# A two-layer diffusion backbone on one core: another order of loads and another sum of squares at its beginning

## The chip, the cores and the metric

The kernel runs on one core of a Trainium2 chip. Its time is the device time of one execution in microseconds (us), the median of several runs; smaller is better. The profile shows one execution, instruction by instruction, for the engines PE (TensorE matmul), PEld (TensorE weight load, which overlaps PE), DVE (VectorE), ACT (ScalarE), POOL (GpSimd) and SP (SyncE, which here only issues DMAs).

## The reference, cut to what matters

Two layers work on 256 latent and 256 context tokens of width 1024. Only the first half-step of the first layer matters here: a norm over the 1024 features of each token, a modulation with a scale and a shift that are themselves matrix products of a condition vector, and a gated FFN.

```python
def _rms(x, g):
    xf = x.astype(jnp.float32)
    y = xf * lax.rsqrt(jnp.mean(xf * xf, axis=-1, keepdims=True) + RMS_EPS)
    return (y * g.astype(jnp.float32)).astype(x.dtype)

def _half_ffn(x, gain, shift, scale, gate, w_gu, w_down):
    h = _rms(x, gain) * (1 + scale) + shift
    a, u = jnp.split(h @ w_gu, 2, axis=-1)
    return x + 0.5 * gate * ((jax.nn.silu(a) * u) @ w_down)
...
m_lat = [m[:, None, :] for m in jnp.split(jax.nn.silu(c) @ w_ada[l] + b_ada[l], N_MOD, axis=-1)]
```

## The kernel before

All is kept transposed: features on the 128 partitions, the 512 tokens (256 latent, then 256 context) along the free dimension, so that x is eight tiles of 128x512, one for each k of 0 to 7. A product in fp32 quality is made of three fp32r matmuls: the weight and the activation are split into a high and a low part, and `mm3` (L341 to L343) multiplies high by high, high by low and low by high. The weight's parts are made on the fly: a raw unit of 128x2048 lands in `raw`, ACT copies 512 columns of it to `whi` (L242), DVE subtracts to get `wlo` (L243). `Weights.piece` does that for a quarter of a unit; a quarter holds the weights for two k. The activation's parts are made by `split` (L346 on ACT, L347 on DVE).

What the first matmuls of the FFN need is made in `start` and `first`:

- `start` issues all early DMAs on SP, in the order x (eight of 256 KB, L398), the constants `cst` (L400, which hold the identity and a block of ones), `vec` (L401), and then `w_ada` for the modulation of feature block 0, 1 (L286, 1 MB each), the first raw unit (L219, 1 MB), `w_ada` 2, the second raw unit, `w_ada` 3 to 7.
- ACT squares the eight tiles of x (L429), DVE adds them into two running sums and these into `acc` (L432, L434). PE multiplies four 128-column slices of `acc` by one column of ones (L441, four matmuls of 128x1): that is the sum over the partitions. DVE turns it into the norm's factor with eleven small instructions (`rsqrt`, L353 to L362).
- `nbc` spreads the factor: two matmuls of 128x128 for each half of the tokens (L588), then an ACT copy out of the bank into `rb` in SBUF (L593).
- `first(j)` makes scale and shift of feature block j: eight matmuls on 32-column groups (L466), an ACT copy (L469), two matmuls with the selector `sel` (L471), two small DVE instructions into `mods` (L475, L476).
- `first_h(k)` makes the FFN's input of block k: DVE multiplies x by `rb` (L484), ACT applies scale and shift to the latent and the context half (L487, two instructions), `split` makes the two parts.

`first(0)` and `first(1)` are called in `start`; the FFN's first loop then runs over k: `first_h(k)`, `first(k + 2)`, and the matmuls of two weight units at once, twelve for each k, into four banks. Each engine works through its instructions in one fixed order; that order is settled when the program is built, by a scheduler which knows priorities and data dependences. A DMA waits for the eighth before it on the same kind of queue to land, since there are eight semaphores that take turns.

## Time and profile before

| | us |
|---|---|
| median of 3 runs | 2036.82 (2030.58 to 2037.09) |
| the profiled execution | 2033.4 |
| its span in the profile | 2031.7 |
| PE busy in the span | 1999.8 (98%) |
| DVE busy | 1394.2 (69%) |
| ACT busy | 884.0 (44%) |

PE is idle for 32 us of the span, and the largest piece of that lies at its start. Times of PE's instructions are read as distances between starts: matmuls overlap, so the duration of one is longer than its share of the engine. The column PEclk is the granted clock as a share of full speed, 1.00 for 2.4 GHz and 0.50 for 1.2 GHz. In the first stretches it reads 1.00 throughout, but the same 128x512 matmuls follow one another every 0.43 us until about 27 us and every 0.23 us from about 29 us on, which are the two levels; there the distances tell the level, not the column.

### The profile page before, as it was taken

To read this page: it belongs to the slowest core of one execution; us is meant where nothing else is said; L and a number is where in the kernel's file an instruction comes from. 1 tells how busy PE (TensorE), PEld (TensorE's weight loads), DVE (VectorE), ACT (ScalarE), POOL (GpSimd) and SP (SyncE) were. 2 spreads that over 40 slices of the span, in tenths; PEclk is the share of its full clock that TensorE was granted. 3 is DMA by queue.
4 is the path that set the end of the run, shared out by engine and by line. 5 is a ranking of instruction groups with operands and counts; after the bars stand their busy time and mean duration, and the time that the engine had idled before them with its cause. 6 is when DMAs were issued, how large, how long until landed. Compare 5 with 4: busy or idle time off the path is not lost.

```text
span 2031.7 us, 30903 instructions
## 1 busy us (share of the span) xinstructions
PE 1999.8 (98%) x12019; PEld 1751.9 (86%) x12019; DVE 1394.2 (69%) x2729; ACT 884.0 (44%) x1683; POOL 22.8 (1%) x49
## 2 busy tenths in 40 slices
PE   7999999999999999999999999999999999999997
PEld 4888888998888888988888898888889889999997
DVE  4999833577458746999933489933346877887675
ACT  4432333456453334532233353223335656466563
POOL 0000000000001000000000000000000000000000
PEclk9999999999999999999999999999999999999999
DMA  9566532324322464466732336532232434455553
GB/s 365 188 227 237 201 101 96 133 89 153 135 89 78 151 233 167 150 240 216 256 122 85 113 122 236 191 121 88 91 127 106 165 135 141 158 206 181 183 174 107
DMA packets 65125, 322.87 MB, mean 159 GB/s; under 512 B 7233, under 2 KB 9681, under 8 KB 36433
## 3 DMA queue, kind: packets, MB, share of 16 engines
q1 hardware_dynamic: 58896, 309.87, 43.9%
q10 hardware_dynamic: 6048, 11.01, 1.5%
q8 instruction: 94, 1.54, 0.3%
q14 instruction: 55, 0.44, 0.1%
q0 software_dynamic: 32, 0.01, 0.0%
HBM read 301.46 MB, written 19.40 MB: 158 GB/s over the span
## 4 chain that ended last, share of the span: by engine, by line
PE 92%; DVE 3%; DMA 2%; ACT 2%; issue 1%; SPq 0%; DVEq 0%; POOLq 0%; ACTq 0%
PE bank L341 28%; PE bank L342 27%; PE bank L343 27%; DMA raw<-in_w_out 1%; PE bank L1209 1%; PE bank L791 1%; PE bank L793 1%; PE bank L792 1%; PE bank L1237 1%; PE bank L1220 1%; DVE wlo L243 0%; PE bank L1236 0%; PE bank L1106 0%; DMA raw<-in_w_in 0%; PE bank L977 0%
## 5 line engine op out<-in xcount | busy, mean ns | idle before, releaser
L341 PE MATMUL bank<-blk,whi 128*128 128x512 f32 (+3 forms) x3064 | 1066.6, 349 | 3.2 <-ACT blk L346 2.6
L342 PE MATMUL bank<-blk,whi 128*128 128x512 f32 (+3 forms) x3064 | 1060.2, 346 | 0.4 <-DVE blk L347 0.3
L343 PE MATMUL bank<-blk,wlo 128*128 128x512 f32 (+3 forms) x3064 | 1059.0, 346 | 0.0
L243 DVE TENSOR_TENSOR wlo<-raw,whi 128x512 fp32r<-128x512 f32 (+2 forms) x748 | 500.5, 678 | 330.0 <-ACT whi L242 326.6
L242 ACT ACTIVATE whi<-raw 128x512 fp32r<-128x512 f32 (+2 forms) x748 | 458.7, 622 | 612.5 <-PE bank L342 564.2
L341 PEld LDWEIGHTS bank<-blk,whi 128*128 128x128 f32 (+1 forms) x3064 | 579.7, 189 | 79.0 <-issue 3.4
L342 PEld LDWEIGHTS bank<-blk,whi 128*128 128x128 f32 (+1 forms) x3064 | 580.4, 190 | 71.1 <-DVE blk L347 1.1
L343 PEld LDWEIGHTS bank<-blk,wlo 128*128 128x128 f32 (+1 forms) x3064 | 580.2, 189 | 70.9 <-DVE wlo L243 0.3
L523 DVE CUSTOM_DVE_ANT_0 blk<-blk,blk,vec 128x1024 f32<-128x1024 f32 x256 | 327.7, 1280 | 2.7 <-DMA blk<-in_w_ada 0.3
L346 ACT ACTIVATE blk<-blk 128x512 fp32r<-128x512 f32 (+2 forms) x128 | 71.5, 560 | 70.6 <-DVE blk L644 49.6
L347 DVE TENSOR_TENSOR blk<-blk,blk 128x512 fp32r<-128x512 f32 (+2 forms) x128 | 76.8, 601 | 27.1 <-ACT blk L346 24.7
L643 ACT ACTIVATE blk<-bank 128x512 f32<-128x512 f32 x66 | 39.5, 598 | 112.6 <-PE bank L343 112.6
L644 DVE TENSOR_TENSOR blk<-blk,bank 128x512 f32<-128x512 f32 x66 | 45.2, 685 | 53.4 <-PE bank L343 53.3
L664 DVE SCALAR_TENSOR_TENSOR blk<-bank,mods,blk 128x256 f32<-128x256 f32 x112 | 50.4, 479 | 33.3 <-PE bank L343 33.3
L342 PE MATMUL bank<-blk,blk 128*128 128x256 f32 (+1 forms) x195 | 58.6, 303 | 0.0
L343 PE MATMUL bank<-blk,blk 128*128 128x256 f32 (+1 forms) x195 | 58.2, 302 | 0.0
L341 PE MATMUL bank<-blk,blk 128*128 128x256 f32 (+1 forms) x195 | 57.9, 304 | 0.0
L498 ACT ACTIVATE blk<-blk 128x256 f32<-128x256 f32 (+1 forms) x55 | 26.1, 474 | 54.1 <-DVE blk L664 36.7
L342 PEld LDWEIGHTS bank<-blk,blk 128*128 128x128 f32 x195 | 37.1, 191 | 1.5
L343 PEld LDWEIGHTS bank<-blk,blk 128*128 128x128 f32 x195 | 37.0, 191 | 1.3
L341 PEld LDWEIGHTS bank<-blk,blk 128*128 128x128 f32 x195 | 36.5, 191 | 1.5
L607 ACT ACTIVATE blk<-blk,mods 128x256 f32<-128x256 f32 x64 | 34.9, 589 | 3.7 <-DVE blk L606 3.7
(254 smaller groups left out, 1395.5 us busy)
## 6 DMA issues: line engine op xcount, KB each, us to landing
raw<-in_gu SPq DMA_DIRECT2D x88, 1024.0 KB, 4.9
blk<-in_w_ada SPq DMA_DIRECT2D x72, 1024.0 KB, 4.8
raw<-in_dn SPq DMA_DIRECT2D x64, 704.0 KB, 4.1
raw<-in_w_in SPq DMA_DIRECT2D x42, 1024.0 KB, 4.8
raw<-in_w_out SPq DMA_DIRECT2D x8, 1024.0 KB, 6.8
dx<-blk SPq DMA_DIRECT2D x16, 256.0 KB, 2.2
raw<-in_w_a SPq DMA_DIRECT2D x4, 1024.0 KB, 6.1
raw<-in_pm SPq DMA_DIRECT2D x3, 1024.0 KB, 4.8
```

The lines of the kernel that those rows point to most:

```text
L242: self.nc.scalar.activation(h[:, a:b], r[:, a:b], AF.Copy)
L243: self.latest = self.nc.vector.tensor_tensor(lo[:, a:b], r[:, a:b], h[:, a:b].bitcast(F32), ALU.subtract)
L341: mm(o, wh, xh, start=start, stop=False)
L342: mm(o, wh, xl, start=False, stop=False)
L343: mm(o, wl, xh, start=False, stop=stop)
L346: self.nc.scalar.activation(hi, src, AF.Copy)
L347: return self.nc.vector.tensor_tensor(lo, src, hi.bitcast(F32), ALU.subtract)
L523: v.tensor_tensor_reduce(self.junk.f, w[:, 1024 * i:1024 * i + 1024], self.cb.f[:, 1024 * s:1024 * s + 1024], 1.0, ba, ALU.mult, ALU.add, ...
L607: nc.scalar.activation(t.f[:, c], t.f[:, c], AF.Identity, bias=self.mod(l, ms, i, s), scale=self.mod(l, mg, i, s))
L643: nc.scalar.activation(t.f[:, :n], o[0][:, :n], AF.Silu)
L644: nc.vector.tensor_tensor(t.f[:, :n], t.f[:, :n], o[1][:, :n], ALU.mult)
L664: nc.vector.scalar_tensor_tensor(self.x[m].f[:, c], p[:, c], self.mod(l, gm, m, s), self.x[m].f[:, c], ALU.mult, ALU.add)
```

## The change

The FFN's loops stay as they are. What changes lies in `start`, `first_h` and the order of loads:

- x comes from two queues: tiles 0, 2, 4, 6 are issued by SP, tiles 1, 3, 5, 7 by ACT.
- The loads after x stand in another order: `cst`, `w_ada` 0, `vec`, the first halves of both raw units, `w_ada` 1, the second half of the first unit, `w_ada` 2, the second half of the second unit, `w_ada` 3 to 7.
- ACT's table is loaded for a one-column Silu that needs no DMA; the Silu of the condition comes after the squares.
- ACT squares tiles 0, 2, 4, 6, DVE tiles 1, 3, 5, 7. DVE adds only two pairs (4 with 5, 6 with 7). The other sums are made by PE: each of the six terms is multiplied by the column of ones in four matmuls, all accumulated in one bank (24 matmuls instead of four).
- The norm's factor is spread by four matmuls into one bank of its own (`banks[7]`), and L499 of the new kernel (L484 before) reads it from there. The two ACT copies are gone.
- In `first_h` the context half gets its scale and shift from DVE (L501), not ACT.

```diff
-            self.nc.sync.dma_start(r[:, :n], ap)
+            h = n // 2 if u < self.halves else n
+            self.nc.sync.dma_start(r[:, :h], ap[:, :h])
...
-            nc.sync.dma_start(self.x[k].f, I["x"][:, k])
+            (nc.scalar if k % 2 else nc.sync).dma_start(self.x[k].f, I["x"][:, k])
...
-        nc.sync.dma_start(self.vec[:, :V_N], I["vec"][:, :V_N])
...
-            if k == 1:
+            if k == 0:
+                nc.sync.dma_start(self.vec[:, :V_N], I["vec"][:, :V_N])
                 self.W.open(self.raw[:1], list(zip(self.whi, self.wlo)))
-            elif k == 2:
                 self.W.more(self.raw[1])
+            elif k < 3:
+                self.W.rest(k - 1)
...
+        nc.vector.memset(self.tiny[:, 0:1], 0.0)
+        nc.scalar.activation(self.tiny[:, 1:2], self.tiny[:, 0:1], AF.Silu)
...
-        self.acc, odd = self.A.get(), self.A.get()
-        two = [self.acc, odd]
+
+        ps, sq = self.ax_bank(), []
         for k in range(KD):
-            t = two[k] if k < 2 else self.A.get()
-            nc.scalar.activation(t.f, self.x[k].f, AF.Square)
-            if k > 1:
-                a = two[k % 2].f
-                nc.vector.tensor_tensor(a, a, t.f, ALU.add)
-                self.A.free(t)
-        nc.vector.tensor_tensor(self.acc.f, self.acc.f, odd.f, ALU.add)
-        self.A.free(odd)
+            sq.append(self.A.get())
+            if k % 2:
+                nc.vector.tensor_tensor(sq[k].f, self.x[k].f, self.x[k].f, ALU.mult)
+            else:
+                nc.scalar.activation(sq[k].f, self.x[k].f, AF.Square)
+            if k in (5, 7):
+                nc.vector.tensor_tensor(sq[k].f, sq[k - 1].f, sq[k].f, ALU.add)
+        nc.scalar.activation(st[:, :, 0:2], self.cc.rearrange("p (k s) -> p k s", s=2), AF.Silu)
+        terms = (0, 1, 2, 3, 5, 7)
+        for k in terms:
+            for t in range(4):
+                nc.tensor.matmul(ps[:, t:t + 1], sq[k].f[:, 128 * t:128 * t + 128], self.ones[:, 0:1], start=(k, t) == (0, 0), stop=k == 7, skip_group_check=True)
...
-        ps = self.ax_bank()
-        for t in range(4):
-            nc.tensor.matmul(ps[:, t:t + 1], self.acc.f[:, 128 * t:128 * t + 128], self.ones[:, 0:1], start=True, stop=True)
...
+        self.rb = self.banks[7]
         with self.tc.issue_after(mm.ins):
-            self.nbc(0)
-            self.nbc(1)
+            for t in range(4):
+                c0 = 8 + 4 * (t // 2) + t % 2
+                nc.tensor.matmul(self.rb[:, t * 128:t * 128 + 128], bc(self.tiny[:, c0], 1, 128), self.ident, start=True, stop=True)
...
-        nc.vector.tensor_tensor(t.f, self.x[j].f, self.rb.f, ALU.mult)
-        for s in range(2):
-            c = slice(256 * s, 256 * s + 256)
-            nc.scalar.activation(t.f[:, c], t.f[:, c], AF.Identity, bias=self.mod(0, 0, j, s), scale=self.mod(0, 1, j, s))
+        nc.vector.tensor_tensor(t.f, self.x[j].f, self.rb, ALU.mult)
+        nc.scalar.activation(t.f[:, :256], t.f[:, :256], AF.Identity, bias=self.mod(0, 0, j, 0), scale=self.mod(0, 1, j, 0))
+        nc.vector.tensor_scalar(t.f[:, 256:], t.f[:, 256:], self.mod(0, 1, j, 1), self.mod(0, 0, j, 1), ALU.mult, ALU.add)
```

The lines move by 8 to 15: L441 is L450 afterwards, L466 is L481, L471 is L486, L588 of the beginning is L465, L475 and L476 are L490 and L491, L484 is L499, L487 is L500 (with L501 beside it), L341 to L343 are L349 to L351, L346 and L347 are L354 and L355, L242 and L243 are L250 and L251.

On PE, from the program's first matmul to the FFN's second weight unit, this stood in a row before (`bank_132` and `bank_133` are the first unit's two outputs, `bank_134` and `bank_131` the second's; `cstat` holds the Silu of the condition, and the tiles blk_158 to blk_160 hold w_ada 0 to 2):

```order
L441 MATMUL bank_136<-cst,blk_180 128x1 x4
L466 MATMUL bank_137<-blk_158,cstat 32x256 x8
L588 MATMUL bank_135<-cst,tiny 128x128 x2
L588 MATMUL bank_136<-cst,tiny 128x128
L471 MATMUL bank_137<-cst,blk_180 128x2 x2
L466 MATMUL bank_137<-blk_159,cstat 32x256 x8
L341 MATMUL bank_132<-blk_250,whi_141 128x512
L342 MATMUL bank_132<-blk_252,whi_141 128x512
L341 MATMUL bank_133<-blk_250,whi_141 128x512
...
L466 MATMUL bank_135<-blk_160,cstat 32x256 x8
```

and this stands there now (blk_157 to blk_159 hold w_ada 0 to 2):

```order
L450 MATMUL bank_136<-cst,blk_183 128x1 x16
L450 MATMUL bank_136<-cst,blk_188 128x1 x8
L481 MATMUL bank_137<-blk_157,cstat 32x256 x8
L465 MATMUL bank_138<-cst,tiny 128x128
L486 MATMUL bank_137<-cst,blk_230 128x2 x2
L465 MATMUL bank_138<-cst,tiny 128x128 x3
L349 MATMUL bank_132<-blk_268,whi_141 128x512
...
L351 MATMUL bank_132<-blk_268,wlo_143 128x512
L481 MATMUL bank_135<-blk_158,cstat 32x256 x8
L350 MATMUL bank_133<-blk_270,whi_141 128x512
```

The sum has 24 products instead of four, and `first(1)` (the second L466, now L481 on `bank_135`) has moved from ahead of the FFN's first matmul to behind its sixth. From the 131st of 11,111 PE instructions on (the 151st afterwards) both kernels have the same order on PE to the end.

On DVE, from the first use of the norm's factor on, this stood in a row before (`wlo_143` belongs to the first unit, `wlo_144` to the second; L484 makes the input of a block, L475 and L476 its scale and shift):

```order
L484 TENSOR_TENSOR blk_270<-blk_145,blk_180 128x512
L484 TENSOR_TENSOR blk_362<-blk_145,blk_180 128x512
L484 TENSOR_TENSOR blk_454<-blk_146,blk_180 128x512
L475 TENSOR_SCALAR mods_129<-bank_137,small,vec 128x2
L476 TENSOR_SCALAR mods_129<-bank_137,vec 128x2
L347 TENSOR_TENSOR blk_252<-blk_270,blk_250 128x512
```

and this stands there now:

```order
L499 TENSOR_TENSOR blk_288<-blk_145,bank_138 128x512
L251 TENSOR_TENSOR wlo_143<-raw_139,whi_141 128x512 x2
L501 TENSOR_SCALAR blk_288<-blk_288,mods_129 128x256
L251 TENSOR_TENSOR wlo_144<-raw_140,whi_142 128x512 x2
L355 TENSOR_TENSOR blk_270<-blk_288,blk_268 128x512
L499 TENSOR_TENSOR blk_320<-blk_145,bank_138 128x512
L490 TENSOR_SCALAR mods_129<-bank_135,small,vec 128x2
L491 TENSOR_SCALAR mods_129<-bank_135,vec 128x2
L251 TENSOR_TENSOR wlo_143<-raw_139,whi_141 128x512 x2
L501 TENSOR_SCALAR blk_320<-blk_320,mods_129 128x256
```

Two subtractions of weight parts (L251) now stand between the factor and L501 for the first block, and two more between the scale and shift of the second block (L490, L491) and its L501; before, the four of a unit stood together behind the first block's parts.

## Rows read from the trace of the kernel before

**Rows 1.** Waits of PE, whole span: waiter, releaser, us in total, times, longest.

```profile
PE bank L441 <- DVE blk L434: 12.8, 1, 12.8
```

**Rows 2.** Chain that ended last, 12 to 24 us: start, us, work.

```profile
12.77 1.88 PE bank L441 x8
17.08 1.65 PE bank L588 x6
...
19.37 0.65 PE bank L588 x2
20.05 0.39 ACT blk L593
```

**Rows 3.** Timeline, 4.5 to 21 us: start, us, engine, line, form, [idle before].

```profile
4.57 0.43 SPq L400 DMA_DIRECT2D cst<-in_cst  x1
...
11.87 0.17 DVE L438 TENSOR_SCALAR small<-vec 128x8 f32<-128x8 f32 x1
...
12.77 1.78 PEld L441 LDWEIGHTS bank<-cst,blk 128*128 128x128 f32 x8 [12.77 <-DVE blk L434]
...
14.67 0.16 DVE L443 TENSOR_SCALAR tiny<-bank 128x4 f32<-128x4 f32 x1 [1.96 <-PE bank L441]
...
16.86 0.16 DVE L362 SCALAR_TENSOR_TENSOR tiny<-tiny 128x4 f32<-128x4 f32 x1
...
19.94 1.94 PE L466 MATMUL bank<-blk,cstat 128*32 128x256 f32 x16
```

**Rows 4.** DMA issues around 4.5 us: KB each, us from issue to landing.

```profile
cst<-in_cst SPq DMA_DIRECT2D x1, 160.5 KB, 5.9
```

**Rows 5.** Stretches: length, busy time of PE, PEld, DVE, ACT, POOL; PEclk, DMA share, GB/s.

```profile
35.00:560.00 525.00, 525.00 (x2966) 442.53 (x2966) 365.40 (x690) 220.99 (x392) 4.22 (x8) 1.00 0.46 161
...
2.00:4.00 2.00, 0.00 (x0) 0.00 (x0) 0.00 (x0) 0.00 (x0) 0.00 (x0) 1.00 0.82 237
4.00:6.00 2.00, 0.00 (x0) 0.00 (x0) 0.00 (x0) 0.85 (x1) 0.00 (x0) 1.00 1.03 342
...
10.00:12.00 2.00, 0.00 (x0) 0.00 (x0) 2.00 (x6) 0.82 (x2) 0.00 (x0) 1.00 1.02 431
```

**Rows 6.** Chain that ended last, 672 to 690 us.

```profile
678.06 3.46 PE bank L1280 x24
...
685.99 0.43 PE bank L342
...
686.69 0.23 PE bank L341
```

**Rows 7.** One of the stretches there.

```profile
680.00:682.00 2.00, 2.00 (x10) 1.90 (x10) 0.44 (x2) 0.00 (x0) 0.00 (x0) 0.50 0.75 240
```

**Rows 8.** Timeline, 21 to 35 us.

```profile
23.64 0.80 PE L341 MATMUL bank<-blk,whi 128*128 128x512 f32 x1
...
24.79 0.80 PE L342 MATMUL bank<-blk,whi 128*128 128x512 f32 x1 [0.35 <-DVE blk L347]
...
25.25 2.49 DVE L243 TENSOR_TENSOR wlo<-raw,whi 128x512 fp32r<-128x512 f32 x4
...
34.73 0.61 PE L471 MATMUL bank<-cst,blk 128*128 128x2 f32 x4 [0.50 <-ACT blk L469]
```

**Rows 9.** Groups: line, engine, form, count; busy us, mean ns; idle before, releaser.

```profile
L664 DVE SCALAR_TENSOR_TENSOR blk<-bank,mods,blk 128x256 f32<-128x256 f32 x112 | 50.4, 479 | 33.3 <-PE bank L343 33.3
L475 DVE TENSOR_SCALAR mods<-bank,small,vec 128x2 f32<-128x2 f32 x8 | 2.2, 279 | 9.6 <-PE bank L471 9.6
L346 ACT ACTIVATE blk<-blk 128x512 fp32r<-128x512 f32 x9 | 5.6, 625 | 0.2
```

**Rows 10.** Chain that ended last, 40 to 43 us.

```profile
40.21 1.00 PE bank L466 x16
41.21 0.43 PE bank L342
...
42.34 0.34 PE bank L471 x4
```

More of the change, by code (lines that the diff above doesn't have):

```diff
@@ L164, in __init__ @@
         self.lent = None
+        self.halves = 2
         self.latest = NULL
@@ L174, in open, with rest @@
         self.plan()
+    def rest(self, u):
+        if self.order:
+            r, n = self.at[u][:2]
+            self.nc.sync.dma_start(r[:, n // 2:n], self.src(u)[:, n // 2:])
     def more(self, raw):
@@ L406, in start @@
             self.AW.more(self.abuf[k].f)
-            if k == 1:
+            if k == 0:
+                nc.sync.dma_start(self.vec[:, :V_N], I["vec"][:, :V_N])
                 self.W.open(self.raw[:1], list(zip(self.whi, self.wlo)))
-            elif k == 2:
                 self.W.more(self.raw[1])
+            elif k < 3:
+                self.W.rest(k - 1)
         nc.sync.dma_start(self.cst[:, 321:], I["cst"][:, 321:])
         nc.sync.dma_start(self.vec[:, V_N:], I["vec"][:, V_N:])
+        nc.vector.memset(self.tiny[:, 0:1], 0.0)
+        nc.scalar.activation(self.tiny[:, 1:2], self.tiny[:, 0:1], AF.Silu)
         nc.vector.memset(self.cstat, 0.0)
         st = self.cstat.rearrange("p (k s) -> p k s", s=32)
-        nc.scalar.activation(st[:, :, 0:2], self.cc.rearrange("p (k s) -> p k s", s=2), AF.Silu)
         self.st = st
@@ L424, in start @@
         self.Sr = [self.cstr[:, 128:256], self.cstr[:, 256:384]]
-        self.acc, odd = self.A.get(), self.A.get()
-        two = [self.acc, odd]
+        ps, sq = self.ax_bank(), []
         for k in range(KD):
-            t = two[k] if k < 2 else self.A.get()
-            nc.scalar.activation(t.f, self.x[k].f, AF.Square)
-            if k > 1:
-                a = two[k % 2].f
-                nc.vector.tensor_tensor(a, a, t.f, ALU.add)
-                self.A.free(t)
-        nc.vector.tensor_tensor(self.acc.f, self.acc.f, odd.f, ALU.add)
-        self.A.free(odd)
+            sq.append(self.A.get())
[10 more added lines that the diff above has]
+                nc.tensor.matmul(ps[:, t:t + 1], sq[k].f[:, 128 * t:128 * t + 128], self.ones[:, 0:1], start=(k, t) == (0, 0), stop=k == 7, skip_group_check=True)
+        self.A.free(sq)
         vb = self.vec[:, 0:V_N]
@@ L685, in ffn @@
                     self.AW.close()
-                    A.free(self.acc, self.rb)
                     for i in range(2):
```

## The prediction

> **What bounds the kernel now.** I read the waits first. PE is idle for 32 us of 2031.7, and the first wait, for the last addition of the squares, is 12.8 of them [rows 1]. From the 131st PE instruction on the order on PE is the same in both kernels, and from 35 to 560 us PE is busy without a gap, 525.00 us [rows 5]. So the change is worth what it moves the moment at which PE gets there, and that shift is handed to the end one to one; nothing later can swallow it. In this trace PE gets there at about 58 us. The chain shows what fills the time before [rows 2]: the sum (L441), the factor on DVE, its spreading (L588), the copies, the first block's input, the first FFN matmul at 23.64 us [rows 8]. 0.3%, 6.1 us, is about what a measurement of this kernel can tell from no change.
>
> **The start of the sum.** Before, the products with ones wait for all additions, until 12.77. Now the first needs only the first square and the column of ones, and that lies in `cst`, issued at 4.57 and landing 5.9 us later, at 10.5 [rows 3, 4]. Still all 2 MB of x but a part of the other queue's share lie ahead of it. Issuing from two queues helps only where the DMA engines idle: their share is 0.82 in the stretch from 2 to 4 us, so 0.36 us, and about 1 from 4 us on [rows 5]. I take 10.2 us. Bounds: if two queues raised the rate from 342 GB/s to the 431 that larger rows reach at 10 to 12 us [rows 5], some 1.7 us less, 8.5; if the two queues served `cst` last, 10.9. By then all squares but the last are done, so PE is what follows.
>
> **The sum on PE.** Four products are eight records, 1.88 us in all; their weight loads start (1.78 - 0.29)/7 = 0.213 us apart [rows 2, 3] (0.29 being the shortest load there). That is with the clock at the lower level, 1.2 GHz. Twenty-four products are 48 records: 47 x 0.213 + 0.4 = 10.4 us, so the sum ends at 20.6 where it ended at 14.65: **+6.0**. Would the long stream raise the clock? The trace holds such a stream: L1280 of the mixer, twelve products of the same form, 24 records in 3.46 us [rows 6]. PE was busy without a gap, and the clock fell: the stretch behind it is at 0.50 [rows 7], and the 128x512 matmuls that follow stay 0.43 us apart until 686 us and are 0.23 apart from 686.7 on [rows 6]. So I take the lower level throughout. The Trainium skill, "TensorE: Matmul & The Clock Gate", section "What's actually happening", speaks against this price: activity releases the clock, and what counts is how long it lasts, not how many matmuls it is made of. By that rule the stream would earn the upper level part of the way through, which is the first rival below; the trace disagrees by [rows 7].
>
> **The factor.** From the first to the last of the twelve instructions it is 14.67 to 17.03 [rows 3], and stays so. Two instructions on `vec` (L438 and its neighbour, 0.17 us each, 0.08 apart [rows 3]), which lay under the additions, now stand between them: **+0.2**. `vec` has landed by then: 12.9 us, 1.15 MB behind `cst` at 431 GB/s [rows 5]. The factor is ready at 23.2 instead of 17.04.
>
> **From the factor to the first FFN matmul.** Before, 6.6 us (17.04 to 23.64). Now: spreading and selector 2.95 (17.08 to 20.02 [rows 2], the same matmuls), no copy (-0.39 [rows 2]), the product with x 0.7, then on DVE two weight subtractions at 2.49/4 = 0.62 each [rows 8], then L501. No row has a 128x256 scaling by two columns on DVE; between 0.28 (L475, two columns wide) and 0.48 (L664, which has three operands [rows 9]) I take 0.4, nearer L664, which has the width. Then ACT's high part, 0.62 [rows 9], and some 0.05 for each of five handovers: 6.1, with ACT's own two copies in between 6.3. **-0.3.** The first halves of both raw units stand 2.2 MB behind `cst`, which is 5.1 us at 431 GB/s [rows 5]: they have landed by about 15.3 us, and no load is waited for.
>
> **`first(1)` moves.** Before, its eight matmuls filled 19.94 to 21.88 [rows 3] while PE waited for the copy and the input anyway: they cost nothing. Now they follow the FFN's sixth matmul and take PE's time: 1.00 for the eight, 0.43 instead of 0.23 for the matmul behind them, 0.34 for the selector [rows 10], 0.1 for the switch back. **+1.65.**
>
> **New waits for blocks 1 and 2.** Because `first(1)` comes late, scale and shift of block 1 come late: after its selector matmuls DVE makes them (0.4), then by its order two weight subtractions (1.24), then L501 (0.4), then ACT the high part (0.62), with handovers 2.8 us. PE has three matmuls left, 0.7: it waits 2.1. For block 2 the order has two subtractions and two products with x between the two halves of its scale and shift and L501: 3.9 us against some 2.8 of PE's work, 1.1 to 1.4, and then 0.6 for the low part. In all 3.9 to 4.1. In the old order PE lost 1.15 - 0.43 = 0.7 between its first two FFN matmuls and 0.5 before L471 [rows 8]. **+2.8.** This is the least sure term: 1.0 to 3.3.
>
> **The clock behind the start.** Before, the lower level lasted until about 27.4 us, 3.8 us after the first FFN matmul. After L1280 it took from 681.5 to 686.4, 4.9 us [rows 6]. I take the same for both kernels, 0; the 1.1 us of difference at half speed would cost 0.6, and a new pause that falls into the rise up to 1.
>
> The rest has one answer: ACT's early table load, the four issues on ACT and DVE's squares end before `cst` lands, nobody waits for them, 0. If `cst` came at 5 us, the squares would pace the sum instead, and the products would still take their 10.4 us.
>
> **Sum:** 6.0 + 0.2 - 0.3 + 1.65 + 2.8 = +10.3 us. On the profiled execution, 2033.4, that is 2043.7; on the median, 2036.82, 2047.1. The profiled execution lies inside the spread of the runs (2030.58 to 2037.09), so I take the middle, 2045.5. With the bounds (start -1.7 to +0.7, waits -1.8 to +0.5, clock 0 to +1) the shift is +7 to +12.5.
>
> **Rivals.**
> 1. *The stream raises the clock.* If the clock rose some 4 us after the first product, as after the first FFN matmul, the last 29 records would be half as far apart, -3.1 us; the factor's spreading (2.95) would save 1.3, and the first FFN matmuls the 1.5 that they lose at the lower level. About +4.5: 2040, within 0.3%. For it: PE is busy for 10 us. Against it: [rows 6, 7], and PE worked from 17.08 to 21.88 without a gap [rows 2, 3] and was still at 1.2 GHz after it.
> 2. *The sum keeps pace with the loads*: not slower. Its place is PE between the landing of `cst` and the last square. If the products of the first squares were done when x's last tile is added (about 11.5 us), only four would follow, 1.9 us: 13.4 instead of 14.65, -1.25; with -0.3 for the copies, -1.2 for the old waits and -4 for a clock that is up from the first FFN matmul on, -6.8: 2029. It decides at the distance of the records: for the sum to end before 14.65 the 48 must be less than (14.65 - 10.2)/48 = 0.093 us apart, and even at the upper level the same loads are 0.11 apart (half of 0.213).
> 3. *The change doesn't bring what it says about loads*: x no earlier from two queues, `cst` last. That is the upper bound of the first term, +0.7, with the same sign as the forecast.
>
> **How the numbers follow.** Forecast 0.78 (its upper bound holds the third rival), clock rival 0.13, sum that keeps pace 0.05, 0.04 for something else that hides the start. In the forecast's case some 0.08 of 0.78 falls below 6.1 us. Slower by over 0.3%: 0.72; within: 0.22 (0.08, the clock rival, a part of the rest); faster: 0.06. The range takes the shift from +3.5 on 2034 to +12.5 on 2037: 2037.5 to 2049.5; the clock rival lies in it, the second rival outside.
>
> **What would show it.** In the changed kernel's chain: L450 with 48 records over about 10 us from about 10 us on; the factor (last L370) near 23; the first L349 near 29.5; PE waiting some 2 us for L354 of block 1 near 36; the end of the common start near 68 instead of 58. The prediction fails if L450's records are 0.11 apart, if L450 ends before 15 us, or if PE doesn't wait between 35 and 46 us.

## The result, and the profile after

The changed kernel takes 2048.62 us (median of 6 runs, 2046.27 to 2054.08) beside 2036.57 us of the kernel before (6 runs). The two medians are 12.05 us apart; the ratio on record, worked out over the runs of both, is 1.0069, with an interval of 1.0052 to 1.0087, so 10.6 to 17.7 us slower. The forecast was 2045.5, from 2037.5 to 2049.5: this median lies 0.9 us below the upper end, and the median of a second set of runs (e11 below), 2050.38, lies above it. The profiled execution is the one of 2046.27 us, span 2044.6, against 2033.4 and 2031.7: +12.9. The sum of the prediction was +10.3. The sign and most terms hold; the 2.6 us that are missing come from one term, the clock behind the start, less what three others came out smaller.

To measure a start, I take one instruction behind it, the first copy of the FFN's first output from its bank (L643 before, L657 after). Its group's line in each trace holds the moment of the first one behind the duration:

```profile
L643 ACT ACTIVATE blk<-bank x66: 597/598/601, 56.7 to 1485.4; 128x512 f32<-128x512 f32 x66
```

```profile
L657 ACT ACTIVATE blk<-bank x66: 587/598/601, 69.2 to 1499.8; 128x512 f32<-128x512 f32 x66
```

From 56.7 to 69.2: the start is longer by 12.5 us, and nothing later swallows it (the falls of the clock further on, told below, happen to cost both traces some 5 us, which is luck). I call this moment the end of the start; the table below uses it for every kernel. (A record is an entry of the trace; an fp32 product on PE leaves two, an fp32r matmul of the FFN one. Chunk j is the scale and shift of feature block j, made by `first(j)`.)

The waits of PE up to 70 us (waiter, releaser, us in total, times, longest), which answer [rows 1]:

```profile
PE bank L450 <- ACT cstat L446: 9.5, 1, 9.5
PE bank L349 <- ACT blk L354: 6.3, 3, 3.0
PE bank L350 <- DVE blk L355: 0.8, 1, 0.8
PE bank L465 <- DVE tiny L370: 0.6, 1, 0.6
```

The wait ahead of the sum is shorter by 3.3 us than the 12.8 of [rows 1], as the change means it to be. In its place stand three waits for the high part of a block's input (L354): 3.0 ahead of the first block, 2.0 and 1.3 ahead of the next two. With the one for the low part of block 2 (L355) they stand in the timeline of PE, the wait in brackets:

```profile
36.50 0.73 PE L349 MATMUL bank<-blk,whi 128*128 128x512 f32 x2 [2.02 <-ACT blk L354]
...
43.47 0.73 PE L349 MATMUL bank<-blk,whi 128*128 128x512 f32 x2 [1.28 <-ACT blk L354]
...
45.88 0.80 PE L350 MATMUL bank<-blk,whi 128*128 128x512 f32 x1 [0.77 <-DVE blk L355]
```

The issue of the constants, and one stretch, which answer [rows 4, 5]:

```profile
cst<-in_cst SPq DMA_DIRECT2D x1, 160.5 KB, 4.4
```

```profile
4.00:6.00 2.00, 0.00 (x0) 0.00 (x0) 0.69 (x1) 1.11 (x3) 0.00 (x0) 1.00 1.03 379
```

The timeline of the factor and of the first FFN matmul (the last step of the factor; the first FFN matmul with the idle time before it):

```profile
22.09 0.16 DVE L370 SCALAR_TENSOR_TENSOR tiny<-tiny 128x4 f32<-128x4 f32 x1
...
28.27 2.07 PE L349 MATMUL bank<-blk,whi 128*128 128x512 f32 x4 [3.03 <-ACT blk L354]
```

And the stretches in which most of the missing time lies (length; busy time of PE, PEld, DVE, ACT, POOL; PEclk; DMA share; GB/s):

```profile
42.00:44.00 2.00, 0.71 (x6) 0.48 (x3) 1.89 (x4) 1.31 (x3) 0.00 (x0) 1.00 1.03 295
44.00:46.00 2.00, 1.23 (x8) 0.76 (x6) 1.27 (x4) 0.60 (x1) 0.00 (x0) 0.83 0.56 234
46.00:48.00 2.00, 2.00 (x17) 0.77 (x17) 1.44 (x3) 0.63 (x1) 0.00 (x0) 0.50 0.00 0
48.00:50.00 2.00, 2.00 (x13) 1.25 (x5) 0.69 (x1) 0.38 (x1) 0.00 (x0) 0.50 0.00 0
50.00:52.00 2.00, 2.00 (x8) 1.77 (x7) 0.82 (x3) 0.65 (x2) 0.00 (x0) 0.50 0.00 0
52.00:54.00 2.00, 2.00 (x21) 1.03 (x19) 0.69 (x1) 0.58 (x1) 0.00 (x0) 0.96 0.00 0
```

PE waits for 1.28 us at 42.2 and for 0.77 at 45.1; from about 45.3 to 52.2 us the granted clock is 0.50, the lower level. The chain there shows it in the matmuls themselves (start, us, work):

```profile
46.68 1.87 PE bank L481 x16
...
51.83 0.43 PE bank L350
52.26 0.24 PE bank L351
```

The sixteen records of a chunk take 1.87 us, where they take 1.00 at the upper level [rows 10], and the 128x512 matmuls stand 0.43 us apart up to 51.83 and 0.24 behind it. PE worked at that level from 45.9 to 52.2; 6.3 us at half speed cost 3.2.

**Busy and idle PE up to the end of the start** (the same columns; the first number behind the length is PE's busy time):

```profile
0.00:56.70 56.70, 41.74 (x264) 28.61 (x265) 27.63 (x67) 29.57 (x59) 0.88 (x5) 1.00 0.82 327
```

```profile
0.00:69.20 69.20, 52.02 (x304) 38.11 (x305) 30.16 (x74) 23.48 (x44) 0.88 (x5) 0.95 0.70 268
```

Before, PE worked for 41.7 us and stood still for 15.0; after, it worked for 52.0 and stood still for 17.2. Of the +10.3 us of work 8.5 are the products (10.4 for 1.9); the 3.2 of the clock are in it too, and the other work took some 1.4 less. The pause ahead of the sum shrank by 3.3 us, and yet PE stood still for 2.2 us more.

### The profile page after: what moved, and what is told of

The parts are those of the page before. It is cut to its first block, busy times and chain, and to the rows that moved or that the text cites. A ratio compares the mean times of both kernels' runs of the same rounds, so it can differ in the third digit from the quotient of the medians.

```text
span 2044.6 us, 30977 instructions
## 1 busy us (share of the span) xinstructions
PE 2010.5 (98%) x12059; PEld 1761.2 (86%) x12059; DVE 1396.8 (68%) x2737; ACT 878.3 (43%) x1670; POOL 22.8 (1%) x49
## 4 chain that ended last, share of the span: by engine, by line
PE 90%; DVE 4%; DMA 2%; ACT 2%; issue 1%; SPq 0%; DVEq 0%; ACTq 0%
PE bank L349 27%; PE bank L350 27%; PE bank L351 27%; DVE wlo L251 1%; DMA raw<-in_w_in 1%; PE bank L1222 1%; PE bank L1250 1%; PE bank L804 1%; PE bank L450 1%; PE bank L1233 1%; ACT whi L250 0%; PE bank L806 0%; PE bank L805 0%; PE bank L1249 0%; DMA dyb<-blk 0%
## 5 line engine op out<-in xcount | busy, mean ns | idle before, releaser
L349 PE MATMUL bank<-blk,whi 128*128 128x512 f32 (+3 forms) x3064 | 1066.6, 349 | 8.7 <-ACT blk L354 6.3
L351 PE MATMUL bank<-blk,wlo 128*128 128x512 f32 (+3 forms) x3064 | 1060.0, 346 | 0.6 <-DVE wlo L251 0.6
L251 DVE TENSOR_TENSOR wlo<-raw,whi 128x512 fp32r<-128x512 f32 (+2 forms) x748 | 500.5, 678 | 330.9 <-ACT whi L250 326.2
L250 ACT ACTIVATE whi<-raw 128x512 fp32r<-128x512 f32 (+2 forms) x748 | 458.8, 622 | 612.8 <-PE bank L350 564.5
L349 PEld LDWEIGHTS bank<-blk,whi 128*128 128x128 f32 (+1 forms) x3064 | 579.1, 189 | 85.8 <-ACT blk L354 7.9
L351 PEld LDWEIGHTS bank<-blk,wlo 128*128 128x128 f32 (+1 forms) x3064 | 580.1, 189 | 71.8 <-DVE wlo L251 0.8
L354 ACT ACTIVATE blk<-blk 128x512 fp32r<-128x512 f32 (+2 forms) x128 | 71.5, 560 | 72.8 <-DVE blk L658 50.0
L355 DVE TENSOR_TENSOR blk<-blk,blk 128x512 fp32r<-128x512 f32 (+2 forms) x128 | 76.7, 601 | 21.0 <-ACT blk L354 18.5
L657 ACT ACTIVATE blk<-bank 128x512 f32<-128x512 f32 x66 | 39.5, 598 | 114.8 <-PE bank L351 114.8
L351 PE MATMUL bank<-blk,blk 128*128 128x256 f32 (+1 forms) x195 | 58.2, 302 | 0.0
L349 PE MATMUL bank<-blk,blk 128*128 128x256 f32 (+1 forms) x195 | 57.8, 304 | 0.0
L351 PEld LDWEIGHTS bank<-blk,blk 128*128 128x128 f32 x195 | 37.0, 191 | 1.3
L349 PEld LDWEIGHTS bank<-blk,blk 128*128 128x128 f32 x195 | 36.5, 191 | 1.5
```

Source lines behind the costliest of these rows:

```text
L250: self.nc.scalar.activation(h[:, a:b], r[:, a:b], AF.Copy)
L251: self.latest = self.nc.vector.tensor_tensor(lo[:, a:b], r[:, a:b], h[:, a:b].bitcast(F32), ALU.subtract)
L349: mm(o, wh, xh, start=start, stop=False)
L351: mm(o, wl, xh, start=False, stop=stop)
L354: self.nc.scalar.activation(hi, src, AF.Copy)
L355: return self.nc.vector.tensor_tensor(lo, src, hi.bitcast(F32), ALU.subtract)
```

## The experiments

All kernels on one page: the end of the start in the profiled execution, its shift against the kernel before (56.7), and the ratio of the times with its interval. The ratios hold more than the start: single falls of the clock further on, at about 497 to 520, 677 to 704 and 1630 to 1820 us, one or more of them in every trace, the kernel before included, in places that change. So the shift is the sharper measure, though it is that of one execution each.

| kernel | end of the start | shift | ratio |
|---|---|---|---|
| changed kernel | 69.2 | +12.5 | 1.0069 (1.0052 to 1.0087) |
| changed kernel, second trace (e11) | 73.4 | +16.7 | 1.0070 (1.0056 to 1.0084) |
| new sum alone (e2) | 63.8 | +7.1 | 1.0042 (1.0029 to 1.0056) |
| loads alone (e7) | 57.6 | +0.9 | 1.0017 (1.0009 to 1.0026) |
| changed, old sum (e1) | 60.9 | +4.2 | 1.0019 (1.0006 to 1.0032) |
| changed, chunk 1 first (e3) | 64.1 | +7.4 | 1.0060 (1.0045 to 1.0075) |
| the same, second trace (e12) | 63.0 | +6.3 | 1.0044 (1.0031 to 1.0057) |
| changed, waits filled (e4) | 67.2 | +10.5 | 1.0061 (1.0044 to 1.0078) |
| before, filled ahead of the sum (e5) | 59.5 | +2.8 | 1.0017 (1.0003 to 1.0031) |
| e3, filled ahead of the sum (e6) | 65.8 | +9.1 | 1.0056 (1.0039 to 1.0073) |
| e1, factor's steps first (e8) | 58.5 | +1.8 | 1.0000 (0.9990 to 1.0011) |
| e8, every engine in the chain's order (e9) | 54.9 | -1.8 | 0.9992 (0.9982 to 1.0003) |
| e9, filled (e10) | 52.4 | -4.3 | 1.0003 (0.9991 to 1.0015) |

**The new sum alone (e2).**

```diff
 # kernel before
-            nc.scalar.activation(t.f, self.x[k].f, AF.Square)
-            if k > 1:
-                nc.vector.tensor_tensor(a, a, t.f, ALU.add)
+            if k % 2:
+                nc.vector.tensor_tensor(sq[k].f, self.x[k].f, self.x[k].f, ALU.mult)
+            else:
+                nc.scalar.activation(sq[k].f, self.x[k].f, AF.Square)
...
+        for k in (0, 1, 2, 3, 5, 7):
+            for t in range(4):
+                nc.tensor.matmul(ps[:, t:t + 1], sq[k].f[:, 128 * t:128 * t + 128], self.ones[:, 0:1], ...)
```

> The kernel before with one part of the change alone: squares on two engines, summed by 24 products into one bank; queue, load order, the copy of the bank for the factor and TensorE's order after it stay as before. Theory A: the products take 48 records of about 0.215 us, 10.4 us, and the sum ends at about 20.9 us where it ended at 14.7 (+6.2); first(1) still stands ahead of the FFN's first matmul, so no new waits of 2 to 3 us at 36 and 43 us and no second fall of the granted clock: +6 us on the kernel before, 2041 to 2044 us. Rival B (order of the loads and of the work is the cost): within 2 us of the kernel before.

The timeline of that kernel, PE:

```profile
10.22 10.37 PE L437 MATMUL bank<-cst,blk 128*128 128x1 f32 x48 [10.22 <-DMA cst<-in_cst]
```

The 48 records take 10.4 us, the sum ends at 20.6 and the end of the start is 7.1 us later. There are no waits of over 1.4 us behind the sum and no fall of the clock. So 7.1 us, measured beside 12.5 for the whole change, are the new sum, with nothing else changed: theory A, a little above its +6. At the first FFN matmul it is 6.5 us (30.09 for 23.64); the rest is the clock, which rises some 5 us behind that matmul here and rose 3.8 behind it before.

**The loads alone (e7).**

```diff
 # kernel before
-            nc.sync.dma_start(self.x[k].f, I["x"][:, k])
+            (nc.scalar if k % 2 else nc.sync).dma_start(self.x[k].f, I["x"][:, k])
...
-            nc.sync.dma_start(r[:, :n], ap)
+            h = n // 2 if u < self.halves else n
+            nc.sync.dma_start(r[:, :h], ap[:, :h])
```

> The kernel before with the loads of the changed kernel alone: x from two queues, the constants and the weights in the changed order and the first two weights in halves, ScalarE's table loaded early; the sum on ScalarE and VectorE with four products, the factor copied from the bank and the splits as before. Theory A (the loads were never what the start waited for, and a part of what they bring forward is spent by VectorE's weight splits that now stand between the steps of the factor): the first FFN group ends 1 to 4 us later than in the kernel before, 0 to +4 us. Rival B (the loads bring what they reach earlier, about 1.5 us for x and 0.8 us for the constants): 1 to 2 us below the kernel before.

+0.9 us, and a ratio above 1: the loads bring nothing, and rival B is out. Why is seen in the next kernel, which has the same order on DVE.

**The changed kernel with the old sum (e1).**

```diff
 # changed kernel
-        for k in (0, 1, 2, 3, 5, 7):
-            for t in range(4): ... 24 products
+            nc.scalar.activation(t.f, self.x[k].f, AF.Square)
+            if k > 1:
+                nc.vector.tensor_tensor(a, a, t.f, ALU.add)
+        for t in range(4): ... 4 products of the sum
```

> The changed kernel with the sum of squares as before: ScalarE squares all eight blocks, VectorE adds them into one tile, four one-column products follow; the two queues, the order of the loads, the bank-read factor and the halved splits stay. Theory A (the sum by 24 products is the cost): the 48 records of 10.37 us on TensorE become 8 records of 1.88 us, so the factor is ready some 6 to 8 us earlier; the weights of blocks 1 and 2 are then split before the FFN reaches them, the waits at 36, 43 and 46 us shrink, and the granted clock does not fall a second time. The first matmul of chunk 1's first tile after the first FFN groups (69.2 us in the changed kernel, 56.7 in the one before) starts at 54 to 58 us, the time is 10 to 15 us below the changed kernel's (2034 to 2038 us). Rival B (the order of the loads and of TensorE's work is the cost, the sum is beside it): within 3 us of the changed kernel, that start above 66 us.

The end of the start is 8.3 us earlier than in the changed kernel: rival B (the order is the cost, the sum is beside it) is out. But theory A's way there is wrong as well (it had the end at 54 to 58 us and no second fall): the factor is ready at 22.2 us, as late as in the changed kernel. Its timeline, DVE and PE:

```profile
12.24 0.17 DVE L451 TENSOR_SCALAR small<-vec 128x8 f32<-128x8 f32 x1 [1.41 <-DMA vec<-in_vec]
...
12.40 0.68 DVE L446 TENSOR_TENSOR blk<-blk 128x512 f32<-128x512 f32 x1
...
15.81 0.16 DVE L457 TENSOR_SCALAR tiny<-bank 128x4 f32<-128x4 f32 x1 [0.89 <-PE bank L454]
...
18.37 0.28 DVE L491 TENSOR_SCALAR mods<-bank,small,vec 128x2 f32<-128x2 f32 x1 [2.41 <-PE bank L487]
...
18.70 0.16 DVE L361 TENSOR_SCALAR tiny<-tiny 128x4 int32<-128x4 int32 x1
...
22.09 0.16 DVE L370 SCALAR_TENSOR_TENSOR tiny<-tiny 128x4 f32<-128x4 f32 x1
```

The last addition (L446) stands behind a step on `vec` that waits 1.41 us for its load; the factor's second step (L361) stands behind chunk 0's step (L491), which waits 2.41 us for PE, and the later ones are mixed with weight splits. What the loads and the old sum gained is lost in DVE's own queue. The 8.3 us come from PE: 8.5 us fewer of products, and chunks 1 and 2 done ahead of the first FFN matmul (28.71), most of it while block 0's input was made. Its clock too fell once, right behind a wait of 0.72 us for that input, from about 28.8 to 35.6 us: 3.4 us. e7, with the same order on DVE, has no such wait and no fall there, and its start ends 3.3 us earlier.

**Chunk 1 ahead of the FFN (e3, and e12 beside a second trace of the changed kernel, e11).**

```diff
 # changed kernel
-        self.first(1)
+        self.mm1 = self.first(1)[0]
...
+                        with self.tc.issue_after(self.mm1.ins) if k == 0 else NULL:
                             for i in range(2):
                                 gu(ws[i], os[i], k, full)
```

> The changed kernel with one order put back: first(1), the 8 records of chunk 1's products, stands ahead of the FFN's first matmul as it did before, all else unchanged. Theory A (the granted clock fell at 45.7 us because of the waits at 36.5 and 43.5 us): the first FFN matmul starts some 1.7 us later, the wait of 2.02 us for block 1 is nearly gone and the one of 1.28 us for block 2 smaller, the clock does not fall again, and the 3.2 us that the lower level cost come back: 3 to 6 us below the changed kernel. Rival B (the fall is not due to these waits): the same work in another order, the waits move but the clock falls all the same: within 1.5 us of the changed kernel.

> The changed kernel once more, unchanged, for a second trace. Theory A (the clock fell at 45.7 us because of the waits at 28, 36.5 and 43.5 us, which the order of the work sets): the same waits within 0.2 us and the same fall, three stretches from 46 to 52 us at 0.50, and the first matmul group of the FFN ends 12 to 13 us later than in the kernel before. Rival B (the fall was an accident of one execution): no fall before 60 us, and that end 9 to 10 us later.

> The changed kernel with chunk 1's products back ahead of the FFN's first matmul, once more, beside the changed kernel. Theory A (without the waits of 2 us the clock stays up): no stretch below 1.00 from the rise up to 60 us, the end of the first FFN groups 4.5 to 5.5 us earlier than in the changed kernel, and the time 3 to 6 us below it. Rival B (the fall is an accident): the two kernels differ there by 1 to 2 us, the waits alone. What the falls further on, which come in other places in each trace, add to the time is open for both.

What is left of the two waits for block 2 in e3:

```profile
41.27 0.73 PE L349 MATMUL bank<-blk,whi 128*128 128x512 f32 x2 [0.37 <-ACT blk L354]
...
43.68 0.50 PE L350 MATMUL bank<-blk,whi 128*128 128x512 f32 x1 [0.78 <-DVE blk L355]
```

The waits of 2.0 and 1.3 us for blocks 1 and 2 are gone or under 0.8. In e3 no stretch is below 1.00 up to 60 us, and the end of the start comes 5.1 us earlier. The ratio doesn't show it; the trace of e3 has some 20 us at the lower level further on, between 1650 and 1700 us. The second trace of the changed kernel has the same waits, but its clock fell twice, for longer than theory A of e11 had it (46 to 52 us), and its start is longer by 16.7 us instead of 12 to 13:

```profile
36.00:38.00 2.00, 0.28 (x1) 0.28 (x2) 1.25 (x4) 0.68 (x2) 0.00 (x0) 0.90 0.51 70
38.00:40.00 2.00, 2.00 (x14) 0.81 (x18) 0.39 (x1) 0.00 (x0) 0.00 (x0) 0.50 0.72 303
40.00:42.00 2.00, 2.00 (x15) 1.15 (x8) 0.00 (x0) 1.13 (x3) 0.00 (x0) 0.74 0.37 156
...
48.00:50.00 2.00, 1.42 (x9) 0.69 (x13) 1.84 (x4) 1.02 (x2) 0.00 (x0) 0.50 0.03 8
...
56.00:58.00 2.00, 2.00 (x18) 0.60 (x16) 0.00 (x1) 0.00 (x0) 0.00 (x0) 0.50 0.00 0
```

PE worked at the lower level from 37.7 to 41.0 and from 48.6 to 58.1 us, 12.8 us in all, which cost 6.4. So both traces fall; what it costs, 3.2 or 6.4 us, changes from one execution to the next, and the end of the start with it (69.2, 73.4). Each of these three falls begins in one of the waits (0.77, 2.02 and 0.78 us). Theory A of e12 holds in the sign; the differences, 10.4 us to the second trace and 7.3 us between the medians (2050.38 and 2043.11), are larger than its 4.5 to 5.5 and 3 to 6. It misses in a detail too, as e12 has the lower level once, from 31.2 to 34.6 us, with PE at work, 1.7 us behind the second of two waits of 1.17 and 0.57 us (at 27.2 and 28.9). Nothing falls from 36 to 60 us in either trace, where the long waits are gone; the 0.78 us that is left did not do it.

**The waits filled (e4).**

```diff
 # changed kernel
+                        with self.tc.issue_after(idle.ins) if 0 < k < 3 else NULL:   # the next block's group behind the fill
...
+                        if k < 2:
+                            with self.tc.issue_after(last.ins):
+                                for _ in range((8, 5)[k]):
+                                    idle = nc.tensor.matmul(b, ws[0][0][:, 0, 0:128], self.hh[0].r, start=True, stop=True)
```

> The changed kernel with 13 matmuls of 128x512 added whose results nobody reads: 8 behind block 0's group of the FFN, 5 behind block 1's, in the time in which TensorE waits for the weights of the next block. Nothing else is moved. Theory A (the granted clock fell at 45.7 us because TensorE stood still at 36.5 and 43.5 us): the clock stays up from its rise at 32 us on, the three stretches from 46 to 52 us show 1.00 in place of 0.50, and the time is about 3 us below the changed kernel's though work is added; the added matmuls may reach past the waits by up to 1 us. Rival B: the clock falls at 45 to 46 us all the same, and the time is the changed kernel's or up to 2 us above.

One of the stretches that were at 0.50, in this kernel, and the first fill:

```profile
46.00:48.00 2.00, 1.25 (x17) 0.60 (x17) 1.84 (x4) 1.19 (x2) 0.00 (x0) 1.00 0.04 12
```

```profile
35.17 1.97 PE L705 MATMUL bank<-blk,whi 128*128 128x512 f32 x8
37.36 0.73 PE L349 MATMUL bank<-blk,whi 128*128 128x512 f32 x2 [0.21 <-ACT blk L354]
```

Work was added, nothing was moved, and the end of the start comes 2.0 us earlier than in the first trace of the changed kernel and 6.2 earlier than in the second. No stretch is below 1.00 up to 60 us; the next block's input comes no earlier (block 1's first matmul starts at 37.36, in the first trace at 36.50). So PE's standing still let the clock fall, and not the order as such, as far as one trace tells it; e6 below is a test from the other side. The gain in the median (2045.85 beside 2048.62) is too small to be told by itself.

**Matmuls ahead of the sum (e5, e6).**

```diff
+        nc.vector.memset(z.f, 0.0)
+        nc.vector.tensor_scalar(z.r, z.f, 1.0, None, ALU.mult)
+        for _ in range(44):        # 30 in e6
+            nc.tensor.matmul(b, z.r[:, 0:128], z.r, start=True, stop=True)
```

> The kernel before with 44 matmuls of 128x512 on a zeroed tile, whose results nobody reads, on TensorE ahead of the sum, in the 12.8 us in which it stands still; nothing else changes. Theory A (the start runs at the lower level because TensorE did nothing before, and keeps the higher one once it is there): the extra matmuls raise the clock within 4 to 6 us, end at about 12.6 us, and the sum, the first chunks and the first FFN groups run at the higher level; the kernel before is at the lower level until about 28 us, with some 13 us of work from 12.8 us on, of which the chain of the factor hides a part: 2 to 5 us below the kernel before. Rival B (the level rises but falls again in the waits of 15 to 24 us): 0 to 1 us below it. Should the extra matmuls not raise the clock, they take 44 x 0.43 = 19 us, the sum starts at 20 us and the time is 7 us above.

> The kernel with the order of first(1) put back, and 30 matmuls of 128x512 on a zeroed tile, whose results nobody reads, on TensorE ahead of the sum by products, in the 9.6 us in which it stands still. Theory A (the products run at whatever level they find and hold it): 48 records at half the distance, 5.2 us in place of 10.4, the sum ends at 15 to 16 us in place of 20.0 and the time is 4 to 6 us below the same kernel without the extra matmuls. Rival B (a stream of one-column products lets the level fall, as at 680 us of the kernel before): the first records are at the short distance and the rest at 0.215 us, sum's end 18 to 20 us, and the time within 1.5 us of the kernel without the extra matmuls.

The kernel before with them (e5), PE, and two stretches:

```profile
2.08 13.01 PE L417 MATMUL bank<-blk 128*128 128x512 f32 x44 [2.08 <-DVE blk L415]
14.94 0.95 PE L447 MATMUL bank<-cst,blk 128*128 128x1 f32 x8
```

```profile
18.00:20.00 2.00, 0.97 (x4) 0.97 (x5) 0.81 (x5) 0.00 (x0) 0.00 (x0) 0.55 1.02 426
20.00:22.00 2.00, 2.00 (x18) 1.32 (x20) 0.44 (x1) 0.77 (x2) 0.00 (x0) 0.50 1.01 422
```

The clock rises (44 matmuls take 13.0 us, where 0.43 us each would be 19) and the sum's eight records take 0.95 us. But 44 were too many: they end at 15.1 us and the sum starts at 14.94, where it started at 12.77 (the last addition comes 0.8 us later here as well). And the level falls at 18 to 20 us, in the wait for the factor, and stays down until 31.9, longer than without them (27.4). That is rival B's way, with a loss of 2.8 us.

The new sum behind 30 of them (e6):

```profile
10.93 5.41 PE L456 MATMUL bank<-cst,blk 128*128 128x1 f32 x48
```

```profile
16.00:18.00 2.00, 2.00 (x20) 0.86 (x19) 1.34 (x9) 0.00 (x0) 0.00 (x0) 0.59 0.99 408
```

The 48 records take 5.41 us, 0.11 apart, the distance at which the prediction's second rival would still not decide. That is theory A's half: here the stream kept the level that it found, for 5.4 us. But the level is gone right behind it, at 16 to 18 us, with PE busy throughout. In the kernel before it went earlier, inside L1280's stream: its 24 records took 3.46 us [rows 6], 0.144 each, between the two distances. Of the 5 us only 2.2 reach the first FFN matmul (26.17, where it was 28.40 in e3): DVE's order puts weight splits between the steps, and the factor is ready at 21.6.

The end of the start is later than in e3 even so (65.8 beside 64.1), and the reason is a second fall. In this trace the waits for block 2 are back, and the clock falls in the second of them, at 40.3 us:

```profile
38.26 0.73 PE L349 MATMUL bank<-blk,whi 128*128 128x512 f32 x2 [1.29 <-ACT blk L354]
...
40.92 0.80 PE L350 MATMUL bank<-blk,whi 128*128 128x512 f32 x1 [1.02 <-DVE blk L355]
```

```profile
40.00:42.00 2.00, 1.08 (x5) 0.49 (x9) 1.84 (x6) 1.23 (x2) 0.00 (x0) 0.56 0.18 74
```

It stays down until 50.5 us, 9.6 us of work, 4.8 us. So e3's order on PE with waits of 1.0 to 1.3 us falls there, and with 0.4 and 0.8 us (e3, e12) it does not.

**The order on each engine (e8, e9, e10).**

```diff
 # e1; e8:
+        self.W.hold = lambda: self.tc.issue_after(self.root.ins)   # weight splits, chunk 0's steps: behind the factor
 # e9, besides:
+        with self.W.hold(): nc.vector.tensor_scalar(self.ba1, vb[...], 1.0, None, ALU.add)   # vec's steps too
+            with self.tc.issue_after(self.pm.ins) if j == 0 else NULL:     # the sum's products ahead of chunk 0's
+                    self.W.held = lambda: self.tc.issue_after(self.gate0.ins)   # later weight splits: behind block 0's parts
...
+                    with self.tc.issue_after(self.half.ins):               # chunk 1's steps behind block 0's scaling
+                        self.mods1()
```

> The changed kernel with the sum of squares as before, and on VectorE the eleven steps of the factor put ahead of the first weight splits and of chunk 0's two steps, which stood between them and made the factor ready at 22.2 us though the sum ended at 15.8. Theory A (that order cost 4 us): the factor is ready at 18.1 us, the first FFN matmul starts at 24 to 26 us in place of 28.7, TensorE has no wait over 3 us behind the sum, and the time is 2 to 5 us below the same kernel without this order, at most 1 us from the kernel before or below it. Rival B (the splits only move behind the factor and are missing there; the FFN's start waits for them instead): within 1 us of the same kernel without this order.

> The changed kernel's loads, bank-read factor and halved splits with the old sum, and an order on each engine that leaves no step of the factor behind another's wait: on VectorE the last addition ahead of the two steps on vec (which held it for 1.7 us), the eleven steps of the factor ahead of the weight splits, block 0's scaling ahead of chunk 1's two steps (which held it for 2.7 us); on TensorE the sum's products ahead of chunk 0's. Theory A (the start is a chain through four engines, and what an engine's order puts between its steps is added to it): the sum ends at 13 to 14 us, the factor is ready at 15.5 to 16.5, the first FFN matmul starts at 19 to 21 us where it was 23.6 in the kernel before and 25.7 with the factor's steps first alone; the time is 2 to 5 us below the kernel before. Rival B (by then the loads of the weights and of chunk 1 set the pace): the first FFN matmul starts early but waits of 1 to 2 us for later blocks follow, and the time is within 1 us of the kernel before.

> The same kernel with 47 matmuls of 128x512 on a zeroed tile, whose results nobody reads: 32 ahead of the sum, 15 in the waits between the sum and the first FFN matmul. Theory A (the level that 44 of them raised fell again in the waits of 16 to 19 us, and without these waits it holds): no stretch at 0.50 up to 60 us, the first FFN groups at the short distance of 0.23 us from the first on, 2 to 4 us below the same kernel without them. Rival B (they stand in the way of the chain, or the level falls all the same): the same or up to 3 us above it.

e8: the factor is ready at 18.5 us and the first FFN matmul starts at 25.68, 3.0 earlier than in e1; the end of the start is 2.4 earlier. Both kernels run their first FFN matmuls at the lower level for some 5.6 to 6.8 us (here from 25.7 to about 31.3, by the distances), so the clock makes little of that difference. The ratio is 1.0000 for 1.0019, which is theory A's way. Two lines of its timeline say where it still stuck:

```profile
24.17 0.28 DVE L495 TENSOR_SCALAR mods<-bank,small,vec 128x2 f32<-128x2 f32 x1 [1.39 <-PE bank L490]
...
24.49 0.41 DVE L506 TENSOR_SCALAR blk<-blk,mods 128x256 f32<-128x256 f32 x1
```

Block 0's scaling (L506) could have run from 22.8 us on, when DVE came free; it stands behind chunk 1's step, which waits for PE. e9 takes that out, and the wait for `vec` too:

```profile
11.70 1.86 PE L457 MATMUL bank<-cst,blk 128*128 128x1 f32 x8 [11.70 <-DVE blk L450]
...
15.79 0.16 DVE L374 SCALAR_TENSOR_TENSOR tiny<-tiny 128x4 f32<-128x4 f32 x1
...
22.19 2.05 PE L353 MATMUL bank<-blk,whi 128*128 128x512 f32 x4
```

The factor is ready at 16.0 (17.04 before), the first FFN matmul starts at 22.19 (23.64 before; 19 to 21 expected: PE's spreading of the factor and chunk 1's products and selector lie between), and the end of the start is 1.8 us earlier than in the kernel before. e10 fills the waits with 47 matmuls and has no stretch below 1.00 up to 60 us: 4.3 us earlier. In the ratios only e9 shows it, and not beyond doubt (0.9982 to 1.0003); e10's runs spread from 2029.47 to 2040.53. The mean granted clock of every run is on record, and it tells where e10's gain went. What the recorded lower level costs a run can be estimated as one minus that clock, times the span: 13.7 us on the mean for e10's twelve runs (clocks of 0.990 to 0.996; the one with the trace has 0.996), 10.7 for the 23 runs of the kernel before beside them. Without that share e10's runs are 3.3 us below those, and e9's 2.4. So most of the gain is in the times, and 3.0 us more of falls, which the one run with a trace doesn't have, hide it; why e10's runs fall more is open.

## Why the prediction was right or wrong

**The start of the sum** was 9.47 us, not 10.2. With the changed loads the rate from 4 to 6 us was 379 GB/s, where [rows 5] has 342, and `cst` landed after 4.4 us, where it took 5.9 [rows 4], so at about 9.3 (the profile puts the start down to ACT's Silu, which ends just then). The bound of 8.5 held it; the middle took too little of the rate: -0.7. Whether the second queue or the order raised the rate isn't shown: no run has one without the other.

**The sum on PE** is right to the digit: 48 records, 10.37 us in the chain, 0.213 apart, at the lower level all the way. The first rival (the stream raises the clock) did not happen in any of the six traces in which this sum follows a PE at rest (two of the changed kernel, e2, e3, e4, e12). The rule of the Trainium skill, "TensorE: Matmul & The Clock Gate", section "What's actually happening", against which the prediction set [rows 7], would have had the level rise within the stream; these traces disagree, by 10.37 us for 48 records.

**The factor** took 2.4 us from the sum's end, as before: +0.0 for +0.2, because the two steps on `vec` fitted between steps that wait for each other. **From the factor to the first FFN matmul** it was 22.25 to 28.27, 6.0 for 6.3. The first FFN matmul is thus 4.6 us later than in the kernel before, where the prediction had 5.9.

**`first(1)` and the new waits**: `first(1)` took 1.8 us of PE's time for 1.65 (1.24 for its eight products, 0.2 for the matmul behind them, 0.35 for the selector). The waits are 2.02, 1.28 and 0.77 us for 2.1, 1.1 to 1.4 and 0.6 (which add up to 3.8 to 4.1, not 3.9 to 4.1). Right, each in its place and for the reason given, DVE's order.

**The clock behind the start** is the step that failed. The prediction took 0 for it, the same in both kernels, with a bound of 1 us for a new pause that falls into the rise. But the waits that it had itself worked out for 34 to 46 us do more than delay a rise: they take the level away again after it has been reached, for 6.3 us of work in the first trace and 12.8 in the second: 3.2 and 6.4 us. Both traces with the waits fall there, and so does e6, where they are back; e4 (the waits filled, 2.0 us earlier though work is added) and e3 and e12 (the long waits gone) don't fall from 36 to 60 us. So the waits are the cause as far as six traces show it, and not only by argument. They are not the only one: the clock also falls with PE at work, inside L1280's stream before and behind the 48 records of e6. The sum with the measured terms: 10.3 - 0.7 - 0.2 - 0.3 + 3.2 = 12.3, for a measured 12.5; in the second trace 3.2 us more for the falls and 1.2 because the first rise came at 34.1 instead of 31.7 us, 16.7 for a measured 16.7. In the trace of before the waits behind the rise are of 0.5 us [rows 8], and the level stays. For waits of 1 to 2 us there was no row; the term should have been bounded by the work that follows them at the lower level, and not by 1 us.

The runs without a trace agree in size, but not in place. By the estimate used for e10 the recorded lower level costs the twelve runs of the changed kernel 14.5 us on the mean, and the runs of the kernel before 10.7 to 11.9 in their four sets: some 3 us more. But the twelve runs of e3 and e12 lose 14.5 as well, and their traces show it further on, between 1650 and 1700 us, with no reason that a run shows.

**What it is made of.** The prediction gave the sum 6.0 us and the displaced order 4.45. By e2 the sum alone is 7.1, and by e3 the order of chunk 1 is worth 5.1, clock included, against the first trace (10.4 for e12 against the second). That the loads, taken alone, bring nothing (+0.9 in e7) stood in the forecast only as the third rival; e9, which has the old sum, shows that with the factor read from its bank they can, once each engine's order lets them.

The second rival (the sum keeps pace with the loads) was priced rightly as far as e6 goes: even at the upper level the records are 0.11 apart.

## What to carry to other kernels

A wait that a change adds has two prices: its length, and the clock level behind it; where PE has just come up, price the second one too. Where a start is a chain through four engines, look at what stands in each engine's queue between two steps of the chain, waits of strangers above all, before a step is made faster: here the changed loads were worth 1.8 us of the start in the right order and less than nothing in another (+0.9 and +4.2). And work that moves from engines that wait to the engine that bounds the kernel is paid for: 8.5 us of products were 7.1 us at the end.

## What the runs showed of the hardware

- The granted clock went from the upper to the lower of its two levels (2.4 and 1.2 GHz) in or right behind waits of 0.7 to 2.0 us (three falls in the changed kernel, one each in e1, e5 and e6). In all of these but e5 it came back after 3.3 to 9.6 us of work without a gap. It stayed up through waits of 0.8 us in e3, e12 and e9. It also fell with PE at work, inside L1280's stream and behind the 48 records of e6. The same program fell in other places and for other lengths in two executions.
- Forty-eight records of one-column products behind a PE at rest stayed at the lower level for 10.4 us; behind 30 wide matmuls they ran at the upper level for 5.4 us, and the level fell behind them.
- With x issued from two queues and another order of loads behind it, all queues moved 379 GB/s in the stretch from 4 to 6 us, where they moved 342; which of the two did it isn't shown.
